# Another order for the change of rounds and the end of a seven-product down projection

## The chip, the cores and the metric

The kernel runs on one core of one Trainium2 chip. The metric is device microseconds (us) of one execution of the program. Five engines work side by side, each in the order of its own queue: TensorE (PE in the profile, with its weight loads as PEld), VectorE (DVE), ScalarE (ACT), GpSimd (POOL) and SyncE (SP), which here issues most DMAs. TensorE writes to PSUM, which has eight banks of 512 fp32 values per partition. The other tiles lie in SBUF.

## The reference

A decoder block on 512 tokens with D = 1024 in fp32: an input projection, sliding-window attention beside a gated linear recurrence, their merge and `w_out`, and then the part that this change touches:

```
h = h + merged @ w_out
u = rmsnorm(h, norm_ffn_g)
z = silu(u @ w_ffn_gate) * (u @ w_ffn_up)        # 512 x 2816
h = h + z @ w_ffn_down                           # 2816 x 1024
return rmsnorm(h, norm_final_g)
```

## The kernel before

**Precision.** Every fp32 product is made of three fast matmuls: each operand is cut into a high half (rounded, made by a copy) and a low half (the remainder, made by a subtraction), and high x high, high x low and low x high are added up in PSUM. For weights the high half `wh` is a copy on ACT (L112) and the low half `wl` a subtraction on DVE (L116).

**Weights.** The class `Weights` brings all weights in as *units* of 1 MB (raw tiles of 128 x 2048, two buffers, loads issued by SP) and cuts each unit into two *slices* (granules in the code) of 128 x 1024, whose halves have three buffers. `get` hands out the next slice and sees that the splits of the next two (`AHEAD`) have been written down before. A split also writes down the load of the next unit. Before a down-projection slice is split, `sums` (L124) adds weight rows on DVE where the method below needs it; in the second round only rows with an even number need it, the first slice of each unit.

**The order on the engines.** The program is written down in one order, and a planner with a cost model of its own decides in which order each engine's queue gets its instructions, by what it believes to be ready when. `tc.issue_after(x)` makes the instructions that stand in its block follow x in the queue of x's engine.

**The FFN.** The rows of h are in `hn` (four token tiles t of 128 rows). For each of the two column halves c of `w_out`, DVE adds the product to hn (L842), PE transposes sixteen 128 x 128 blocks (L845) into PSUM banks `px`, and ACT and DVE write the high and low halves `u2h` (L850) and `u2l` (L851) for k = 4c to 4c + 3. The row factors of the norm are not multiplied in; `row_scale` spreads them with one matmul (L885) into a tile `R`, which is multiplied in later. A projection `fproject` is 24 matmuls (three for each k of 8) from one slice. The hidden width is handled in eleven pairs p = 0..10: `gate(p)` does two projections, `up_(p)` two more and multiplies (`place`, L925), and then builds sums and differences of the parts of z ("forms").

**Seven products.** The down projection treats z and the weights as 2 x 2 blocks (token halves by neighbouring hidden blocks; neighbouring hidden blocks by column halves), and computes the four output blocks from seven block products instead of eight. Each product of a pair p is six matmuls: two token tiles by three. In *round 1*, `round1(p)` accumulates three of them (s3y3, a22y4, s2y2, two banks each) between the projections, over all p. *Round 2* then accumulates the other four (a11b11, n1y1, a12b21, n4b22, two banks each) over p = 0..7, and the loop `tail` does the last three p product by product, so that the output tiles are done one after another. The z forms of round 2, `zh` and `zl`, are kept in SBUF; the forms of round 1 are `f1h`, `f1l`.

**The change of rounds** (L961 to L992). The pool of the projections is given back (L961), a new one is laid over it, two tiles `evs` in it take a copy of s3y3 (ACT), DVE adds a22y4 and s2y2 to hn and to evs, evs is added to hn (four additions, L985 to L987), and then all eight banks are laid out anew for round 2.

**The end.** After each last product, DVE adds it to hn (`onto`, L973; `add_side`, L1035, in pieces of 256 columns), ACT squares the pieces and sums them up. `finish_row(t, late)` multiplies by the gains on POOL (L1044: 512 columns and then 256), reduces on DVE (L1046), takes the power -1/2 on POOL (L1048) and scales by the row's factor: 512 columns on ACT, 256 on DVE (L1050), the last 256 on DVE with the gains (L1051). Then two DMAs write the row tile, one from ACT's queue and one from SP's. Row tiles 2 and 3 are finished first, then 0, then 1.

Of the kernel before, what the change touches and what calls it, by code (L numbers as in the profile page):

```python
# [15 lines left out]
F32 = mybir.dt.float32  # L16
# [6 lines left out]
P = 128  # L23
# [18 lines left out]
class Weights:  # L42


    def __init__(self, nc, pool, units):
        self.nc, self.pool = nc, pool
        self.units = units
        self.raw = {}
        self.grans = []
        for u, (kind, *_rest) in enumerate(units):  # L50
            self.grans += [(u, kind, 0), (u, kind, 1)]
        self.ready = {}
        self.done = 0
        self.pos = 0

    def load(self, u):
# [3 lines left out]
        t = self.pool.tile([P, 2048], F32, tag="raw", bufs=2, name=f"raw{u}")  # L60
# [27 lines left out]
    def split(self, i, pool=None, bufs=3, high=None, low=None, low_after=None):  # L88
        u, kind, half = self.grans[i]
        self.load(u)  # L90
        if u:
            self.load(u + 1)
# [8 lines left out]
        size = 1024  # L101
        if kind in ("r1", "r2"):
# [3 lines left out]
        pool = pool or self.pool  # L106
# [37 lines left out]
def block_kernel(ctx: ExitStack, tc: tile.TileContext, x, norm_mix_g, w_in, b_in,  # L144
# [65 lines left out]
    W = Weights(nc, wpool, units)  # L210
# [176 lines left out]

    def mm3(ps, wh, wl, ah, al):

        for k in range(KD):  # L390
            pe.matmul(ps, wh[:, k, :], ah[:, k, :], start=k == 0, stop=False)  # L391
            pe.matmul(ps, wh[:, k, :], al[:, k, :], start=False, stop=False)  # L392
            pe.matmul(ps, wl[:, k, :], ah[:, k, :], start=False, stop=k == KD - 1)  # L393
# [428 lines left out]
    for c in range(2):  # L822
# [18 lines left out]
        for t in range(NT):  # L841
            tt(hn[:, t, cs], pss[t], hn[:, t, cs], ALU.add)  # L842
            for jj in range(4):
                j = 4 * c + jj
                pe.transpose(px[jj][:, t * P:(t + 1) * P], hn[:, t, j * P:(j + 1) * P], ident)  # L845
            jk = rp.tile([P, S], F32, tag="jk", bufs=2, name="jk")
            act(jk, hn[:, t, cs], AF.Square, accum_out=sq2[:, t, c:c + 1])
        for jj in range(4):
            j = 4 * c + jj
            act(u2h[:, j, :], px[jj], AF.Copy, scale=g_ffn[:, j:j + 1])  # L850
            stt(u2l[:, j, :], px[jj], g_ffn[:, j:j + 1], u2h.bitcast(F32)[:, j, :],  # L851
                ALU.mult, ALU.subtract)
# [13 lines left out]
    psum.release()  # L866
    psum = newpool("psf", "left", bass.MemoryType.PSUM)

    def psg(name):
        return psum.tile([P, S], F32, tag="g", bufs=2, name=name)  # L870

# [4 lines left out]
    rounds1 = {n: [psum.tile([P, S], F32, name=f"{n}_{i}") for i in range(2)]  # L876
               for n in ("s3y3", "a22y4", "s2y2")}
    bc = rounds1["s2y2"][1]
    stream_end = len(W.grans) - 1 - 2 * TAIL_P

    def row_scale():
        diag = fp.tile([P, NT, P], F32, tag="zg", bufs=2, name="diag")
        for t in range(NT):
            dve.tensor_scalar(diag[:, t, :], ident, rstd2[:, t:t + 1], None, ALU.mult)
        pe.matmul(bc, ones, diag.rearrange("p t c -> p (t c)"), start=True, stop=True)  # L885
        dve.tensor_copy(R, bc)

    def fproject(then=None):
        wh, wl = W.get(limit=stream_end)
        ps = psg("ps_f")  # L890
        run(mm3(ps, wh, wl, u2h, u2l))
        if then:
            then()
# [4 lines left out]
    def gate(p):  # L898
        gates_of[p] = []
        for a in range(2):  # L900
            zg = fp.tile([P, S], F32, tag="zg", bufs=2, name="zg")
            tt(zg, fproject(row_scale if p == 0 and a == 0 else None), R, ALU.mult)  # L902
# [9 lines left out]
    def up_(p):  # L912
# [6 lines left out]
        def split(h, l, src):  # L919
            act(h, src, AF.Copy)  # L920
            tt(l, src, h.bitcast(F32), ALU.subtract)

# [6 lines left out]
        if p < NP - 1:  # L929
# [3 lines left out]
            split(h1, l1, z8[:, 4:7, :])  # L933
        else:
            split(h1[:, 2], l1[:, 2], s3)
            place(1)
            split(h1[:, 0], l1[:, 0], a22)
# [12 lines left out]
    def round1(p):  # L950
        h, l = forms1.pop(p)
        for names in (("s3y3",), ("a22y4", "s2y2")):
            wh, wl = W.get(limit=stream_end)
            for b, n in enumerate(names):
                f = dict(a22y4=0, s2y2=1, s3y3=2)[n]
                product(rounds1[n], h[:, f], l[:, f], wh[:, b], wl[:, b],
                        p == 0, p == NP - 1)

    for kind, p in ffn:
# [152 lines left out]
```

## Time and profile before

| | us |
|---|---|
| three runs of before | 909.8, 910.02, 913.58 |
| their median | 910.02 |
| the profiled execution's own time | 911.42 |
| its span, from the first to the last instruction | 909.7 |

All durations below come from that one profiled execution; 1.7 us of its own time lie outside the span. In the views, a row of the timeline has the start, the duration, the engine, the line, the operation, the tile written and the tiles read, and in brackets how long the engine had been idle and what ended it. Rows of the windows have the stretch, its length, busy time and number of instructions of PE, PEld, DVE, ACT and POOL, then the granted TensorE clock (1.00 is full), the busy share of the DMA engines and GB/s. Matmuls overlap: a row's duration reaches from its start to its modelled end, while the next one starts earlier. Rows of the waits have the total, the number and the longest.

### The profile page before, as it was taken

What the parts mean: (1) busy time and instruction counts of PE and PEld (TensorE: products, weight loads), DVE (VectorE), ACT (ScalarE), POOL (GpSimd) and SP (SyncE); (2) the same over time, 40 slices, a digit from 0 to 9 for tenths busy, and PEclk for the clock granted to TensorE, in tenths of its full rate; (3) what the DMA queues carried; (4) which work ended last, traced back from release to release, by engine and by line L of the source; (5) the groups of instructions that cost most, each with busy time, mean ns of one, the idle gap of its engine ahead of it and who ended that gap; (6) DMA issues with size and microseconds to landing.
All of it is one profiled execution on the core that took longest, in us unless ns stands there. A gap on an engine that the chain in (4) does not pass through costs nothing.

```text
span 909.7 us, 11255 instructions
## 1 busy us (share of the span) xinstructions
PE 887.8 (98%) x4410; PEld 749.0 (82%) x4410; DVE 556.6 (61%) x843; ACT 396.6 (44%) x646; POOL 153.4 (17%) x150
## 2 busy tenths in 40 slices
PE   8999999999999999999999999999999999997995
PEld 7988889888898988888888878888888888884874
DVE  5677877647484755745335356565655655667567
ACT  6566775645353545215232342333332333332345
POOL 3004534300000000000000002333322223320005
PEclk9999999999999999999999999999999999997998
DMA  7331211232221141222243222344333343343452
GB/s 257 93 93 47 94 47 47 93 93 93 93 84 56 47 139 47 93 93 92 95 163 114 93 93 93 98 134 139 96 136 121 110 139 116 116 138 116 161 210 94
DMA packets 74642, 97.26 MB, mean 107 GB/s; under 512 B 2042, under 2 KB 64604, under 8 KB 74588
## 3 DMA queue, kind: packets, MB, share of 16 engines
q1 hardware_dynamic: 73996, 95.48, 32.3%
q10 hardware_dynamic: 592, 1.05, 0.3%
q8 instruction: 35, 0.57, 0.3%
q14 instruction: 19, 0.16, 0.0%
HBM read 94.43 MB, written 2.10 MB: 106 GB/s over the span
## 4 chain that ended last, share of the span: by engine, by line
PE 87%; DMA 5%; DVE 4%; SPq 1%; issue 1%; ACT 1%; POOL 0%; DVEq 0%; POOLq 0%; ACTq 0%
PE ps_big L391 13%; PE ps_big L392 13%; PE ps_big L393 13%; PE ps_f L391 8%; PE ps_f L392 8%; PE ps_f L393 8%; DMA raw<-in_w_ffn_down_dram 4%; DVE wl L116 2%; PE ps_v L402 2%; PE ps_v L403 2%; PE ps_v L401 2%; PE ps_o L402 2%; PE ps_o L403 2%; PE ps_o L401 2%; PE pv L527 1%; PE s2y L948 1%
## 5 line engine op out<-in xcount | busy, mean ns | idle before, releaser
L112 ACT ACTIVATE wh<-raw 128x1024 fp32r<-128x1024 f32 (+1 forms) x169 | 173.9, 1032 | 368.2 <-PE ps_f L392 149.1
L116 DVE TENSOR_TENSOR wl<-raw,wh 128x1024 fp32r<-128x1024 f32 (+1 forms) x169 | 211.4, 1252 | 115.7 <-ACT wh L112 115.4
L391 PE MATMUL ps_big<-uh,wh 128*128 128x512 f32 x376 | 148.8, 396 | 0.0
L392 PE MATMUL ps_big<-ul,wh 128*128 128x512 f32 x376 | 147.8, 393 | 0.0
L393 PE MATMUL ps_big<-uh,wl 128*128 128x512 f32 x376 | 147.7, 393 | 0.0
L391 PE MATMUL ps_f<-u2h,wh 128*128 128x512 f32 x352 | 137.4, 390 | 0.0
L393 PE MATMUL ps_f<-u2h,wl 128*128 128x512 f32 x352 | 137.0, 389 | 0.0
L392 PE MATMUL ps_f<-u2l,wh 128*128 128x512 f32 x352 | 136.9, 389 | 0.0
L393 PEld LDWEIGHTS ps_big<-uh,wl 128*128 128x128 f32 x376 | 70.7, 188 | 14.2
L392 PEld LDWEIGHTS ps_big<-ul,wh 128*128 128x128 f32 x376 | 70.8, 188 | 13.6
L391 PEld LDWEIGHTS ps_big<-uh,wh 128*128 128x128 f32 x376 | 70.7, 188 | 13.5
L392 PEld LDWEIGHTS ps_f<-u2l,wh 128*128 128x128 f32 x352 | 66.1, 188 | 13.9 <-issue 0.2
L393 PEld LDWEIGHTS ps_f<-u2h,wl 128*128 128x128 f32 x352 | 66.1, 188 | 13.9
L391 PEld LDWEIGHTS ps_f<-u2h,wh 128*128 128x128 f32 x352 | 66.1, 188 | 13.8 <-issue 0.2
L905 POOL TENSOR_TENSOR zg<-zg,sgf 128x512 f32<-128x512 f32 x22 | 38.9, 1766 | 191.4 <-ACT sgf L162 191.4
L124 DVE TENSOR_TENSOR raw<-raw 128x512 f32<-128x512 f32 x44 | 32.5, 739 | 44.0 <-DMA raw<-in_w_ffn_down_dram 43.6
L285 POOL TENSOR_TENSOR r<-ss,neghalf 128x4 f32<-128x4 f32 x8 | 10.1, 1259 | 232.8 <-DVE ss L284 232.8
L902 DVE TENSOR_TENSOR zg<-ps_f,R 128x512 f32<-128x512 f32 x22 | 15.2, 692 | 37.9 <-PE ps_f L393 37.9
L906 POOL TENSOR_TENSOR zg<-zg,R 128x512 f32<-128x512 f32 x22 | 37.4, 1702 | 1.7
L401 PE MATMUL ps_v<-wh,uh 128*128 128x256 f32 x128 | 36.5, 285 | 0.0
L402 PE MATMUL ps_v<-wl,uh 128*128 128x256 f32 x128 | 36.3, 284 | 0.0
L403 PE MATMUL ps_v<-wh,ul 128*128 128x256 f32 x128 | 36.2, 284 | 0.0
(302 smaller groups left out, 1612.5 us busy)
## 6 DMA issues: line engine op xcount, KB each, us to landing
raw<-in_w_in_dram SPq DMA_DIRECT2D x27, 1024.0 KB, 5.1
raw<-in_w_ffn_gate_dram SPq DMA_DIRECT2D x11, 1024.0 KB, 5.1
raw<-in_w_ffn_up_dram SPq DMA_DIRECT2D x11, 1024.0 KB, 5.2
raw<-in_w_ffn_down_dram SPq DMA_DIRECT2D x11, 1024.0 KB, 4.8
raw<-in_w_ffn_down_dram SPq DMA_DIRECT2D x22, 512.0 KB, 4.2
raw<-in_w_branch_attn_dram SPq DMA_DIRECT2D x4, 1024.0 KB, 5.2
raw<-in_w_branch_hgrn_dram SPq DMA_DIRECT2D x4, 1024.0 KB, 4.7
raw<-in_w_out_dram SPq DMA_DIRECT2D x4, 1024.0 KB, 6.4
```

The source lines that it names most:

```text
L112: nc.scalar.activation(hv, src, AF.Copy)
L116: (low or nc.vector).tensor_tensor(lv, src, hv.bitcast(F32), ALU.subtract)
L124: add = lambda o, i0, i1: self.nc.vector.tensor_tensor(o, i0, i1, ALU.add)
L391: pe.matmul(ps, wh[:, k, :], ah[:, k, :], start=k == 0, stop=False)
L392: pe.matmul(ps, wh[:, k, :], al[:, k, :], start=False, stop=False)
L393: pe.matmul(ps, wl[:, k, :], ah[:, k, :], start=False, stop=k == KD - 1)
L401: pe.matmul(ps, ah[:, k0 + k, ts], wh[:, k, :], start=first and k == 0, stop=False)
L402: pe.matmul(ps, ah[:, k0 + k, ts], wl[:, k, :], start=False, stop=False)
L403: pe.matmul(ps, al[:, k0 + k, ts], wh[:, k, :], start=False, stop=last and k == nk - 1)
L902: tt(zg, fproject(row_scale if p == 0 and a == 0 else None), R, ALU.mult)
L905: pool_e.tensor_tensor(zg, zg, sg, ALU.mult)
L906: pool_e.tensor_tensor(zg, zg, R, ALU.mult)
```

## The change

- **Start of the FFN.** The first two projections get their banks from the old PSUM pool and do k = 0..3 before the last token tile of the second column half is transposed (`turn(NT - 1)`, placed behind the first projection's k = 3). Its u2 halves, `row_scale` (in a bank of the tag "s1") and k = 4..7 follow. The pool is changed when the third projection opens its bank (`open_banks`).
- **Round 1's last pair.** a11b11 of p = 0 stands between s3y3 and a22y4, in the two banks of the projections. The other three products of round 2 take over the banks of s3y3, a22y4 and s2y2. The splits of the first two slices of round 2 are held behind the low half of the s2 form on DVE, that of the second one also behind the last copy of s3y3 on ACT, and that of the third slice behind the last addition of s2y2 to evs (`added`).
- **Evictions.** evs lies in the old pool. The four additions of evs to hn move to p = 1. The last pair's round-2 forms (`rest`) move to p = 2, and then the pool is given back and `gfin` is loaded.
- **Raw buffers.** Units 2, 3, 6, 7 and 10 of round 2 use a second pool `wr` of two raw buffers, which lies where u2 was. With it, a split writes down the loads of the next three units. Two of the last six slices use the ordinary three buffers for their halves and four use the pool `wd`, where all six did.
- **The end.** Squares of 512 columns at once, but for the last side of row tile 1. Row tiles 2, 3 and 0 are scaled on ACT alone (two times 512 columns), POOL multiplies all of their columns by the gains, and both DMAs go out from SP's queue; row tile 1 stays as before.

```
@@ Weights
+        self.more, self.more_units = None, ()
+        self.behind = []
     def load(self, u):
+        if u in self.more_units and self.more is None:
+            return
+        pool = self.more if u in self.more_units else self.pool
+        t = pool.tile([P, 2048], F32, tag="raw", bufs=2, name=f"raw{u}")
     def split(self, i, ...):
-        if u:
-            self.load(u + 1)
+        for v in range(u + 1, u + (4 if self.more else 2 if u else 1)):
+            self.load(v)
...
+        with ExitStack() as order:
+            for ins in self.behind:
+                order.enter_context(self.tc.issue_after(ins))
+            self.cut(i, kind, u, half, raw, src, shape, pool or self.pool, bufs, high, low,
+                     low_after)
@@ start of the FFN
         for t in range(NT):
             tt(hn[:, t, cs], pss[t], hn[:, t, cs], ALU.add)
+            if c == 0 or t < NT - 1:
+                turn(t)
...
+    first = []
+    for a in range(2):
+        wh, wl = W.get()
+        first.append((psb([P, S], "ps_f"), wh, wl))
+        for k in range(4):
+            last_ins = mm3k(*first[a], u2h, u2l, k)
+        if a == 0:
+            with tc.issue_after(last_ins):
+                turn(NT - 1)
+            split_u2()
...
+    row_scale()
+    for ps, wh, wl in first:
+        for k in range(4, KD):
+            mm3k(ps, wh, wl, u2h, u2l, k)
@@ up_(p), last pair
-            split(h1[:, 1], l1[:, 1], s2)
-        tt(n4, a12, s2, ALU.subtract)
-        split(zh[:, p], zl[:, p], z8[:, 0:4, :])
+            W.behind = [split_form(h1[:, 1], l1[:, 1], s2)]
+
+        def rest():
+            tt(n4, a12, s2, ALU.subtract)
+            split_form(zh[:, p], zl[:, p], z8[:, 0:4, :])
+
+        if p < NP - 1:
+            rest()
+        return rest
@@ round1(p)
+        ws = [W.get(limit=first_r2 if last else stream_end) for _ in range(2)]
+        one("s3y3", ws[0], 0)
+        if last:
+            acc["a11b11"] = [banks["g"](f"a11b11_{i}") for i in range(2)]
+            acc["w"] = W.get(limit=first_r2)
+            second("a11b11", 0, acc["w"])
+        one("a22y4", ws[1], 0)
+        one("s2y2", ws[1], 1)
@@ change of rounds
     for i in range(2):
-        ev = dp.tile([P, S], F32, tag="ev", bufs=2, name="ev")
-        act(ev, rounds1["s3y3"][i], AF.Copy)
+        ev = fp.tile([P, S], F32, tag="zg", bufs=2, name="ev")
+        last_copy = raw_ins(act(ev, banks["s3y3"][i], AF.Copy))
         evs.append(ev)
+    W.behind.append(last_copy)
...
+        added = raw_ins(tt(evs[i], banks["s2y2"][i], evs[i], ALU.add))
+    acc.update(n1y1=banks["s3y3"], a12b21=banks["a22y4"], n4b22=banks["s2y2"])
+    wr = newpool("wr", "left")
+    W.more = wr
     for p in range(NP - TAIL_P):
+        w = W.get(limit=stream_end) if p else acc["w"]
+        if p:
+            second("a11b11", p, w)
+        else:
+            W.split(W.done)
+            W.behind = [added]
+            W.split(W.done)
+            W.behind = []
+        second("n1y1", p, w)
+        w = W.get(limit=stream_end)
+        second("a12b21", p, w)
+        second("n4b22", p, w)
+        if p == 1:
+            for i in range(2):
+                onto(2 + i, 1, evs[i])
+                onto(2 + i, 0, evs[i], ALU.subtract)
+        if p == 2:
+            rest()
+            fp.release()
...
     for g in range(2 * TAIL_P):
-        W.split(stream_end + 1 + g, wd, 2 * TAIL_P)
+        if g < 2:
+            W.split(stream_end + 1 + g)
+        else:
+            W.split(stream_end + 1 + g, wd, 4)
@@ finish_row(t, late)
-        for hs in (early, ls):
+        last = t == 1
+        for hs in (early, ls if last else sides[late]):
             pool_e.tensor_tensor(y[:, hs], y[:, hs], gfin[:, hs], ALU.mult)
...
         act(y[:, early], y[:, early], AF.Copy, scale=r1)
-        dve.tensor_scalar(y[:, ls], y[:, ls], r1, None, ALU.mult)
-        stt(y[:, rest], y[:, rest], r1, gfin[:, rest], ALU.mult, ALU.mult)
-        for q, hs in ((nc.scalar, early), (nc.sync, sides[late])):
+        if last:
+            dve.tensor_scalar(y[:, ls], y[:, ls], r1, None, ALU.mult)
+            stt(y[:, rest], y[:, rest], r1, gfin[:, rest], ALU.mult, ALU.mult)
+        else:
+            act(y[:, sides[late]], y[:, sides[late]], AF.Copy, scale=r1)
+        for q, hs in ((nc.scalar if last else nc.sync, early), (nc.sync, sides[late])):
             q.dma_start(out2[t * P:(t + 1) * P, hs], y[:, hs])
```

More of the change, by code (lines that the diff above doesn't have):

```diff
@@ L101, in split, with cut @@
         size = 1024
+        with ExitStack() as order:
[3 more added lines that the diff above has]
+                     low_after)
+    def cut(self, i, kind, u, half, raw, src, shape, pool, bufs, high, low, low_after):
+        nc, size = self.nc, 1024
         if kind in ("r1", "r2"):
@@ L840, in block_kernel, with turn @@
             px = [psb([P, S], "px") for _ in range(3)] + [ps1([P, S], "px")]
[L841 to L842 removed]
+        def turn(t):
             for jj in range(4):
@@ L982, in block_kernel @@
     for i in range(2):
[L983 to L999 removed]
+        onto(i, 1, banks["s2y2"][i])
```

150 lines of the change are left out of this document (76 added, 74 removed).

## Prediction

> **What bounds it now.** I read the page first, then the busy time by windows, the waits of PE, and the timeline at each place where PE stood still.
>
> ```profile
> span 909.7 us, 11255 instructions
> ...
> PE 887.8 (98%) x4410; PEld 749.0 (82%) x4410; DVE 556.6 (61%) x843; ACT 396.6 (44%) x646; POOL 153.4 (17%) x150
> ...
> PEclk9999999999999999999999999999999999997998
> ...
> PE 87%; DMA 5%; DVE 4%; SPq 1%; issue 1%; ACT 1%; POOL 0%; DVEq 0%; POOLq 0%; ACTq 0%
> ```
>
> TensorE is the bound: 98% busy, 87% of the chain. No matmul is removed, so only idle PE time and slow PE clock can be won. The clock row shows one dip, in slices 37 and 38 of 40; the windows and PE's waits say where.
>
> ```profile
> 842.00:882.00 40.00, 40.00 (x178) 33.12 (x177) 22.50 (x22) 15.89 (x15) 0.00 (x0) 1.00 0.53 179
> ...
> 824.14:841.78 17.64, 10.96 (x26) 7.13 (x25) 14.23 (x26) 4.99 (x7) 0.00 (x0) 0.61 0.32 113
> ...
> 826.63:828.03 1.40, 1.24 (x5) 0.71 (x5) 1.40 (x4) 0.90 (x1) 0.00 (x0) 1.00 0.00 0
> 828.03:829.90 1.87, 1.18 (x2) 0.46 (x2) 1.87 (x3) 0.42 (x1) 0.00 (x0) 0.50 0.00 0
> ...
> PE a11b L948 <- ACT ev L157: 3.7, 1, 3.7
> ...
> PE a22y L948 <- ACT f1h L157: 2.1, 1, 2.1
> ...
> PE px L845 <- DVE hn L842: 0.8, 1, 0.8
> ...
> PE a11b L1014 <- DVE wl L116: 0.8, 1, 0.8
> ```
>
> In a full stretch (first row) 178 matmuls touch 40 us, two of them only its ends: 40/176.6 = 0.2265 us each. Between 824.14 and 841.78, the change of rounds, 25 matmuls start (one s3y3, six each of a22y4, s2y2, a11b11, n1y1; 26 touch it). At full pace they need 25 x 0.2265 = 5.7 us of the 17.64: **12.0 us lost**, by idle time and by a granted clock of 0.50 from 828.03 on. The other two waits are the boundary to the FFN (px) and the last products (L1014); behind PE's last matmul comes the end of the kernel.
>
> **The change, part by part.** *A, start of the FFN.*
>
> ```profile
> 539.02 1.03 PE L845 MATMUL px<-ident,hn 128*128 128x128 f32 x8
> ...
> 540.09 1.28 DVE L842 TENSOR_TENSOR hn<-ps_o,hn 128x512 f32<-128x512 f32 x2
> ...
> 540.83 1.25 PE L845 MATMUL px<-ident,hn 128*128 128x128 f32 x8 [0.78 <-DVE hn L842]
> ...
> 541.84 0.47 PE L391 MATMUL ps_f<-u2h,wh 128*128 128x512 f32 x1
> ...
> 542.11 2.40 ACT L157 ACTIVATE u2h<-px,prm 128x512 fp32r<-128x512 f32 x4
> ...
> 542.82 1.41 DVE L851 SCALAR_TENSOR_TENSOR u2l<-px,prm,u2h 128x512 fp32r<-128x512 f32 x2
> ```
>
> The sixteen transposes take 541.84 - 539.02 = 2.82 us, against 2 x 1.03 for two groups like the first: 0.8 us is waiting for hn, and some 0.3 more restarting behind it. After the change 24 matmuls on k = 0..3 (two projections, 5.4 us) need only what the first column half left, so PE has work. The last token tile's transposes move behind twelve of them, to about 543.6; its u2h then takes 2.4 us on ACT and its u2l 4 x 0.71 us on DVE, plus the diagonal that DVE already writes there, ending near 548.3. PE asks for k = 4 at about 547.2 and for k = 7 two microseconds later, so each is there in time. The row-scale matmul is the same, in a freed "s1" bank. If that cover failed, late u2l would cost what is won. Gain 0 to 1.1; I take **1.0**.
>
> *B, the change of rounds.*
>
> ```profile
> 822.78 0.39 PE L393 MATMUL ps_f<-u2h,wl 128*128 128x512 f32 x1
> ...
> 824.84 0.69 DVE L124 TENSOR_TENSOR raw<-raw 128x512 f32<-128x512 f32 x1 [3.53 <-DMA raw<-in_w_ffn_down_dram]
> ...
> 825.45 0.68 DVE L925 TENSOR_TENSOR z<-ps_f,zg 128x512 f32<-128x512 f32 x1
> ...
> 826.05 1.22 DVE L116 TENSOR_TENSOR wl<-raw,wh 128x1024 fp32r<-128x1024 f32 x1
> ...
> 826.17 0.42 ACT L157 ACTIVATE f1h<-z 128x256 fp32r<-128x256 f32 x1 [2.08 <-DVE z L925]
> ...
> 826.49 1.04 ACT L112 ACTIVATE wh<-raw 128x1024 fp32r<-128x1024 f32 x1
> ...
> 826.64 0.50 PE L948 MATMUL a22y<-wh,f1h 128*128 128x512 f32 x1 [2.11 <-ACT f1h L157]
> ...
> 834.66 1.22 DVE L921 TENSOR_TENSOR zl<-z,zh 128x1024 fp32r<-128x1024 f32 x1
> ...
> 835.91 1.09 ACT L157 ACTIVATE ev<-s3y 128x512 f32<-128x512 f32 x2 [1.93 <-DVE zl L921]
> ...
> 836.56 0.80 PE L948 MATMUL a11b<-wh,zh 128*128 128x512 f32 x1 [3.72 <-ACT ev L157]
> ```
>
> The last up projection ends at 822.78 + 0.39 = 823.2, yet the product that reads it (L925) starts at 825.45: DVE's queue is headed by a weight sum (L124) that waits for a DMA. That is PE's first gap, 2.27 us from 824.37 to 826.64. The second is the bank: a11b11 waits for ev, and ev, in a pool laid over the old one, for zl.
>
> After the change DVE has no weight work of round 2 in front of the forms. L925 starts at 823.2, f1h 0.72 later (825.45 to 826.17) at 823.9, a22y4 another 0.47 later at 824.4, just as s3y3 ends (824.14 + 0.23). The s2 form needs two subtractions, a copy and a low half, about 0.45 each: done near 825.7. PE does a22y4 and s2y2 to 824.4 + 12 x 0.2265 = 827.1.
>
> The added wait: behind the s2 form's low half, DVE now holds the first round-2 slice's sum (0.69) and low half (1.22); ACT's high half (1.04) needs the sum; a11b11 and n1y1 on PE need all three. Sum to 826.4, high to 827.5 (828.15 if ACT takes the odd row's slice first), low 1.2 later. PE idles 0.4 to 1.0 us, with up to 0.35 more for the low half. Next, the first slice of unit 1 is held behind `added`, behind six evictions of 0.64 (1.28 for two hn additions in A's rows; 3.8 us) and two low halves (2.4 us): from 826.4 that is 832.6, up to 833.1 with the waits between them; then sum and high, 834.3 to 835.0. PE's 24 matmuls from 827.5 end near 833.4. So p = 1 starts at 834.3 to 835.0 instead of 841.78 + 12 x 0.2265 = 844.5. With no idle time it would be 832.5. Of the 12.0 us some 1.8 to 2.5 stay: gain **9.9**, between 9.5 and 12.0.
>
> What moves: four additions of evs to p = 1 (4 x 0.64 = 2.6 us of DVE) and the last z forms to p = 2 (a 256-wide subtraction of about 0.42 and a low half of 1.22 on DVE, a high half of about 1.04 on ACT). In the full stretch above DVE is busy 22.5 of 40 us, ACT 15.9, so about 7 us of DVE are free in the 16 us that take these 4.2; cost nothing, and up to 2 us if they push a low half out of its turn. On SP, the loads of units 2 and 3 go out once u2h is free (823.2) instead of waiting for a split; gfin stands behind them until the old pool is free, with four raw buffers (4 x 24 x 0.2265 = 21.7 us of PE work) as cover.
>
> *C, last products.*
>
> ```profile
> 883.73 0.39 PE L1014 MATMUL a11b<-wh,zl 128*128 128x512 f32 x1
> ...
> 885.77 0.40 PE L1014 MATMUL a11b<-wh,zl 128*128 128x512 f32 x1
> ...
> 881.64 5.14 DMA raw<-in_w_ffn_down_dram
> ...
> 886.81 1.07 ACT wh L112
> ```
>
> From 883.73 to 885.77 three matmuls start in 2.04 us that need 0.68: **1.4** lost to late splits, behind loads that wait for two raw buffers (the chain shows one from 881.64). With four, unit 10's load can go when unit 6 is split, some 6 us ahead of need. Gain 0 to 1.4; I take 1.4.
>
> *D, the end.*
>
> ```profile
> 900.07 0.39 PE L1014 MATMUL n4b<-wh,zl 128*128 128x512 f32 x1
> ...
> 899.69 0.75 POOL L1044 TENSOR_TENSOR hn<-hn,gfin 128x256 f32<-128x256 f32 x1 [1.50 <-ACT jkd L157]
> ...
> 900.90 1.27 POOL L1044 TENSOR_TENSOR hn<-hn,gfin 128x512 f32<-128x512 f32 x1
> ...
> 900.97 0.72 ACT L157 ACTIVATE hn<-hn,r1d 128x512 f32<-128x512 f32 x1 [0.16 <-POOL r1d L1048]
> ...
> 900.97 1.35 DVE L1050 TENSOR_SCALAR hn<-hn,r1d 128x256 f32<-128x256 f32 x1 [0.77 <-POOL r1d L1048]
> ...
> 902.64 0.74 DVE L1035 TENSOR_TENSOR hn<-n4b,hn 128x256 f32<-128x256 f32 x2
> ...
> 904.93 0.35 DVE L1050 TENSOR_SCALAR hn<-hn,r1d 128x256 f32<-128x256 f32 x1 [0.75 <-POOL r1d L1048]
> ```
>
> PE's last result is there at 900.46, but DVE adds it at 902.64: it first scales row 0, where one L1050 takes 1.35 us beside a POOL multiplication that ends at 902.17, against 0.35 without one (904.93). Row 0 goes to ACT, so the add can start 2.1 us earlier. What is late next: POOL multiplies 512 columns where it did 256 for three rows (1.27 - 0.75 = 0.5 each), and row 0's two ACT scalings (1.44) stand before the last squares. From that add to row 1's scaling are 904.93 - 902.64 = 2.29 us of squares, reduction and power; from 900.5 on they end at 902.8 if nothing stands between them, and at 903.2 to 903.9 if row 0's scalings hold the squares back by one (0.72, in part) or both. So 1.0 to 1.7 us; I take **1.2**, bounds 2.1 gained and 0.6 lost (POOL's 1.5 added in full on top of 0.9 kept).
>
> Sum: 1.0 + 9.9 + 1.4 + 1.2 = **13.5 us**. The profiled execution took 911.42 (span 909.7 and 1.7 around it), 1.4 above the median of 910.02; so 897.9 in its terms, **896.5** as a median.
>
> **Rivals.** *One half-clock stretch remains.* A mean clock of 0.61 over the 17.64 us, with 3.89 at 1.00, leaves 0.50 for all the rest: 13.75 us. If B's remaining idle time trips it again in dense work, 13.75/2 = 6.9 us go: 903.4. Against: gaps of 1.0 us (540) and 1.4 us in two parts (884) left the clock alone, and I expect 1.0 at a time; it took a 2.27 us gap here. The Trainium skill, "TensorE: Matmul & The Clock Gate", Part 1, has the clock halve only after an idle window of about 3.4 us. By that rule this rival falls away and its chance goes to the forecast; the trace disagrees, since 2.27 us was enough, and the trace decides.
>
> *ScalarE and POOL become the end.* Row 0's scaling delays the last squares and POOL's added 3 x 0.5 us shows: D costs 0.6 instead of gaining 1.2, 898.3. The Trainium skill, "ScalarE: Activation LUTs", Rules for kernel authors, is on this side: it gives multiplications to VectorE, not ScalarE. The rows are against it where POOL runs: 1.35 for 256 columns on DVE, 0.72 for 512 on ACT.
>
> *It doesn't do what it says*: PE's order keeps a11b11 before a22y4. PE then waits from 824.37 to 827.5, over the 2.27 that tripped the clock, and B gains nothing: only A, C and D count, 906.4.
>
> *Slower*: the clock keeps closing. Round 2 is dense, so each stretch costs 6.9 us; two eat all 13.5 (910.3), a third gives 896.5 + 20.7 = 917.2. It decides from three stretches on. For it: two idle spots 6 us apart; against: the one stretch before was not followed by another.
>
> **How the numbers follow.** Forecast 0.68, one stretch 0.13, end bound 0.08, no effect at B 0.07, slower 0.04. A measurement of this kernel tells about 0.5%, 4.6 us, from no change. Faster 0.68 + 0.13 + 0.08 = 0.89, same 0.07, slower 0.04. Low end: B whole, A 1.1, D 2.1, so 1.1 + 12.0 + 1.4 + 2.1 = 16.6 gained, 893.4; high end the one-stretch rival, 903.4; outside it stay 0.11.
>
> **What would show it.** Right: PE clock 1.00 through the change of rounds, no PE gap over 1.1 us there, p = 1 ten microseconds earlier, L925 within 0.5 us of the last up-projection matmul, no L1014 wait, L1050 only once and at 0.35. Wrong: a clock of 0.50 near 828; DVE's queue headed by a weight sum waiting for a DMA (units 2 and 3 are not held back by order); PE waiting for `wh` over 2 us; POOL without idle time after 895.

## The result and the profile after

| | before | after |
|---|---|---|
| median of four runs | 909.91 us | 903.85 us |
| lowest to highest | 909.77 to 913.58 | 903.16 to 904.19 |
| ratio, 95% interval | | 0.9923, 0.9897 to 0.9948 |
| the profiled execution's span | 909.7 us | 902.1 us |

By the medians the change makes the kernel faster by 6.1 us, 0.7%. The ratio in the table, 0.8% (0.5 to 1.0%), is that of the means, in which before's run of 913.58 counts. The forecast was 896.5 within 893.4 to 903.4: the sign held, the size was less than half, and the time lies 0.45 us above the range.

From the page of the changed kernel, to be read against the page of before:

```profile
span 902.1 us, 11238 instructions
...
PE 886.8 (98%) x4410; PEld 747.6 (83%) x4410; DVE 550.6 (61%) x836; ACT 396.9 (44%) x635; POOL 154.1 (17%) x150
...
PEclk9999999999999999999999999999999999999999
...
PE 91%; DMA 3%; DVE 3%; SPq 1%; issue 1%; ACT 0%; POOL 0%; POOLq 0%; DVEq 0%; ACTq 0%
```

The dip of the clock in slices 37 and 38 is gone from the page, and PE's share of the chain has grown from 87 to 91%. A slice is 22.6 us long, so the clock row can't show a short stretch. The windows of the changed kernel can; the last column but two is the granted clock:

```profile
823.25:836.51 13.26, 9.50 (x30) 6.21 (x29) 13.05 (x22) 5.69 (x8) 0.00 (x0) 0.87 0.49 175
...
826.09:829.50 3.41, 2.23 (x9) 1.08 (x7) 3.41 (x6) 1.96 (x2) 0.00 (x0) 1.00 0.89 344
829.50:832.92 3.42, 0.99 (x2) 0.37 (x2) 3.42 (x5) 0.86 (x1) 0.00 (x0) 1.00 0.02 8
832.92:836.33 3.41, 3.25 (x8) 2.61 (x9) 3.41 (x6) 0.19 (x1) 0.00 (x0) 0.50 0.13 29
...
868.00:880.00 12.00, 11.38 (x46) 8.05 (x46) 9.99 (x9) 7.47 (x8) 0.00 (x0) 1.00 0.26 88
```

In the first row 29 matmuls start (30 touch it). They need 29 x 0.2265 = 6.6 us and take 13.26: **6.7 us are still lost** at the change of rounds, where 12.0 were lost before. From 829.50 to 832.92 PE starts two matmuls, and the 3.41 us behind that run at a clock of 0.50. In the last row 46 matmuls touch the twelve microseconds that hold 54 at full pace (the last row of *turned_tail_free* below): 54 - 46 = 8 matmuls, or 1.8 us, are lost among the last products, where 1.4 were.

What PE waited for from 815 us on, first; then VectorE's and PE's rows of the timeline at the change of rounds:

```profile
PE s2y L1002 <- DVE ev L1054: 2.0, 2, 1.3
PE a11b L1002 <- DVE wl L129: 1.5, 2, 1.2
PE a11b L1002 <- ACT wh L125: 0.5, 1, 0.5
...
```

```profile
822.38 0.69 DVE L969 TENSOR_TENSOR z<-ps_f,zg 128x512 f32<-128x512 f32 x1 [2.82 <-PE ps_f L405]
...
824.36 0.42 DVE L987 TENSOR_TENSOR z<-z 128x256 f32<-128x256 f32 x1
824.93 0.43 DVE L996 TENSOR_TENSOR f1l<-z,f1h 128x256 fp32r<-128x256 f32 x1 [0.15 <-ACT f1h L170]
825.27 0.68 DVE L137 TENSOR_TENSOR raw<-raw 128x512 f32<-128x512 f32 x1
825.88 0.68 DVE L1042 TENSOR_TENSOR hn<-hn,a22y 128x512 f32<-128x512 f32 x1
826.47 0.68 DVE L137 TENSOR_TENSOR raw<-raw 128x512 f32<-128x512 f32 x1
827.08 0.68 DVE L1042 TENSOR_TENSOR hn<-hn,a22y 128x512 f32<-128x512 f32 x1
827.67 1.22 DVE L996 TENSOR_TENSOR zl<-z,zh 128x1024 fp32r<-128x1024 f32 x1
828.81 0.68 DVE L1042 TENSOR_TENSOR hn<-hn,s2y 128x512 f32<-128x512 f32 x1
...
830.60 0.68 DVE L1054 TENSOR_TENSOR ev<-s2y,ev 128x512 f32<-128x512 f32 x1
831.20 0.68 DVE L137 TENSOR_TENSOR raw<-raw 128x512 f32<-128x512 f32 x1
831.80 1.22 DVE L129 TENSOR_TENSOR wl<-raw,wh 128x1024 fp32r<-128x1024 f32 x1
```

```profile
821.89 0.39 PE L405 MATMUL ps_f<-u2h,wl 128*128 128x512 f32 x1
...
827.15 0.73 PE L1002 MATMUL a11b<-wh,zh 128*128 128x512 f32 x2 [0.52 <-ACT wh L125]
...
828.19 0.65 PE L1002 MATMUL a22y<-wh,zh 128*128 128x512 f32 x2
830.15 0.50 PE L1002 MATMUL s2y<-wh,zh 128*128 128x512 f32 x1 [1.30 <-DVE ev L1054]
831.34 0.49 PE L1002 MATMUL s2y<-wh,zh 128*128 128x512 f32 x1 [0.70 <-DVE ev L1054]
833.08 0.80 PE L1002 MATMUL a11b<-wl,zh 128*128 128x512 f32 x1 [1.24 <-DVE wl L129]
```

(In the lines on PE, a11b, s3y, a22y and s2y on zh are a11b11, n1y1, a12b21 and n4b22 of round 2: the banks keep their old names.) VectorE never stops from 824.93 on. It has the forms done early, as forecast, and place(1) (L969) starts as soon as its product is there. But the low half of round 2's first slice (L129) comes at 831.80, behind ten other instructions. Six are the reads of the banks. One is the slice's own sum. The other three were not expected there: the sum of unit 2 (826.47), the low half zl of the last pair (827.67), which the program writes down at p = 2, and the sum of unit 1 (831.20). The planner had pulled them forward. PE has the high-half products of both slices put first, then stands in front of s2y2's banks at 828.7 and 830.4, and in front of the low half at 831.6.

### The profile page after: what moved, and what is told of

It reads as the page before. It is cut to its first block, busy times and chain, and to the rows that moved or that the text cites. A ratio compares the mean times of both kernels' runs of the same rounds, so it can differ in the third digit from the quotient of the medians.

```text
span 902.1 us, 11238 instructions
## 1 busy us (share of the span) xinstructions
PE 886.8 (98%) x4410; PEld 747.6 (83%) x4410; DVE 550.6 (61%) x836; ACT 396.9 (44%) x635; POOL 154.1 (17%) x150
## 4 chain that ended last, share of the span: by engine, by line
PE 91%; DMA 3%; DVE 3%; SPq 1%; issue 1%; ACT 0%; POOL 0%; POOLq 0%; DVEq 0%; ACTq 0%
PE ps_big L405 13%; PE ps_big L403 13%; PE ps_big L404 13%; PE ps_f L404 9%; PE ps_f L405 9%; PE ps_f L403 9%; DMA raw<-in_w_ffn_down_dram 3%; PE ps_v L420 2%; PE ps_v L421 2%; PE ps_v L419 2%; PE ps_o L420 2%; PE ps_o L421 2%; PE ps_o L419 2%; DVE wl L129 2%; PE s2y L1002 2%; PE a22y L1002 2%
## 5 line engine op out<-in xcount | busy, mean ns | idle before, releaser
L129 DVE TENSOR_TENSOR wl<-raw,wh 128x1024 fp32r<-128x1024 f32 (+1 forms) x169 | 209.5, 1245 | 107.2 <-ACT wh L125 106.2
```

What stands on the lines that cost most here:

```text
L129: (low or nc.vector).tensor_tensor(lv, src, hv.bitcast(F32), ALU.subtract)
```

## The experiments

All are edits of the changed kernel, and all compute the whole output. In the count of the whole weight stream, which the expectations use, units 0 to 10 of round 2 are units 74 to 84 and their slices 148 to 169. The ratio is against before, run beside them on the same chip (its medians there are 909.38 to 909.79, beside after 909.91, so a difference to after's median can be off by half a microsecond); "lost" is what PE's steps from one matmul to the next have above 0.2265 us, where that is over 0.08 us, and so a little less than the counts above; "end" is from the start of the last matmul to the end of the span.

| kernel | median us | ratio, 95% interval | lost 820-860 | lost 860-885 | end |
|---|---|---|---|---|---|
| before | 909.91 | | 12.0 | 1.2 | 9.6 |
| after | 903.85 | 0.9923 (0.9897 to 0.9948) | 6.5 | 1.6 | 7.7 |
| rest_late | 899.55 | 0.9894 (0.9878 to 0.9911) | 4.1 | 0.1 | 7.7 |
| sums_late | 901.71 | 0.9916 (0.9901 to 0.9931) | 4.8 | 1.0 | 7.6 |
| evict_late | 900.82 | 0.9906 (0.9892 to 0.9921) | 4.8 | 0.8 | 7.7 |
| splits_free | 898.44 | 0.9881 (0.9866 to 0.9896) | 3.8 | 0.4 | 7.6 |
| sums_in_turn | 903.75 | 0.9937 (0.9923 to 0.9952) | 3.9 | 3.7 | 8.3 |
| all_turned | 898.93 | 0.9882 (0.9868 to 0.9897) | 0.0 | 2.1 | 9.0 |
| turned_tail_free | 895.07 | 0.9839 (0.9823 to 0.9856) | 0.0 | 0.0 | 7.6 |
| turned_scaling_dve | 894.96 | 0.9842 (0.9827 to 0.9857) | 0.0 | 0.0 | 7.5 |
| two_raw | 903.15 | 0.9927 (0.9910 to 0.9943) | 7.3 | 0.8 | 8.4 |
| scaling_on_dve | 903.21 | 0.9930 (0.9915 to 0.9945) | 7.3 | 0.8 | 7.6 |
| small_squares | 903.50 | 0.9933 (0.9918 to 0.9948) | 6.5 | 1.4 | 8.3 |
| old_end | 903.79 | 0.9938 (0.9921 to 0.9954) | 6.7 | 1.1 | 7.7 |

The three losses come from one trace each. How much of that is chance, *scaling_on_dve* shows: VectorE and PE have the same order as in after at the change of rounds, and yet 7.3 us are lost in place of 6.5, because two stretches of 3.41 us at half clock follow in place of one.

The theory to test was that VectorE's order sets the start of round 2, and that whatever stands ahead of the first low half and of the reads of s2y2 is paid in full. The rivals: loads or ScalarE set it; the half clock alone costs.

**rest_late** holds the last pair's remaining forms back:

```
-                onto(2 + i, 0, evs[i], ALU.subtract)
+                held = onto(2 + i, 0, evs[i], ALU.subtract)
...
-            rest()
+            with tc.issue_after(held):
+                rest()
```

> The last pair's n4 and four forms (rest) are held behind the four additions of evs, on VectorE. Theory 1 (VectorE's own order sets the start of round 2: everything that stands ahead of the last two reads of s2y2 and of the first slice's low half is paid in full): zl with 1.15 us a step leaves that place, so the first low half starts at about 830.65 instead of 831.80 and the time falls by 1.1 to 1.2 us to 902.7; if the three gaps of PE also become short enough that no half clock follows, by another 1.6 us (eight products at 0.426 instead of 0.2265 us) to 901.1. Rival 2 (the loads or ScalarE's high halves set the start): no change, 903.9. Rival 3 (only the half clock costs, the gaps are hidden): no change or 902.3.

4.3 us less, more than any theory had. By the traces the change of rounds gave 2.4 of it, close to the 2.8 of the case without a half clock, which is indeed gone. The other 1.5 came from the last products, where nothing had been expected; *sums_in_turn* is about them.

**sums_late** holds the splits of units 75 to 77 behind the first low half:

```
+            low148 = W.low_ins
             W.split(W.done)
-            W.behind = [added]
+            W.behind = [added, low148]
             W.split(W.done)
-            W.behind = []
...
         if p == 1:
+            W.behind = []
```

(`low_ins` is the instruction of the last low half written down.)

> The splits of units 75, 76 and 77 (sum, high and low half) are held behind the low half of the first slice as well as behind the last read of s2y2. Theory 1: the sums of units 76 and 75 (0.60 us a step each) leave the place ahead of the first low half, which starts at about 830.6 instead of 831.8; 1.2 us less, 902.65, or 901.05 without the half clock; the three sums then stand ahead of the second slice's low half, which starts at 833.5 as before. Rival 2 (loads or ScalarE): no change, 903.9. A third outcome is that the third slice's high half, now behind sum 75 at about 832.4, comes too late and gives 0.5 us of it back.

2.1 us less, again without a half clock, between the two values given.

**evict_late** puts the first low half ahead of the reads of s2y2:

```
+    with tc.issue_after(W.low_ins):
         for i in range(2):
             onto(i, 1, banks["s2y2"][i])
             added = raw_ins(tt(evs[i], banks["s2y2"][i], evs[i], ALU.add))
```

> The four instructions that read s2y2 are held behind the low half of the first slice; the sum of unit 76 and the rest of the last pair still stand ahead of it. PE's order changes with it: the eight low products of the first slice come ahead of the two high ones into s2y2's banks. Theory 1: low half from 828.8 instead of 831.8, the eight products from 830.0; the banks of s2y2 free at 831.2 and 832.4; the third slice's high half, behind the sum of unit 75, at about 834: gaps of 0.7, 1.3, 0.4 and 1.4 us in place of 0.7, 1.5, 1.0 and 1.5 with a half clock of 1.6: about 2.4 us less, 901.4 (or 903.1 if a half clock stays). Rival 2 (the banks of s2y2 set the start, since round 2 needs them): these come 1.15 us later, so 1 us slower, 904.9.

3.0 us less, though s2y2's banks come free later: the banks are not the bound by themselves, their place in VectorE's queue is. All three edits take only a different piece out of the same queue, and each gains. The rival that loads or ScalarE alone set the start falls.

**splits_free** undoes one part of the change, the holds of round 2's first splits behind the s2 form, the copies of s3y3 and the reads of s2y2:

```
-            W.behind = [split_form(h1[:, 1], l1[:, 1], s2)]
+            split_form(h1[:, 1], l1[:, 1], s2)
...
-    W.behind.append(last_copy)
...
-            W.behind = [added]
```

> Undoes one part of the change: nothing holds the weight splits behind the forms, the copies or the reads of the banks. VectorE then cuts the first slice between place(1) and the form a22, the second between a22 and s2, and PE has all twelve products of the first slice of round 2 ahead of a22y4. Theory 1 in its wide form (PE idles because the first slice is cut too late; it has nothing else to do while VectorE makes the forms and reads the banks): 2 to 4 us less, about 901. The change's own reason (splits ahead of the forms make the forms late): the forms come 1.2 us later each, place(1) behind the sum of unit 75 that lands at about 823.5 another 1 us: 1 to 3 us more, about 906.

5.4 us less. The part that was to make the start of round 2 early cost that much: with the first slice cut early, PE has its twelve products to do while VectorE makes the forms. What still stands in the way shows in VectorE's timeline of this run:

```profile
823.90 0.69 DVE L137 TENSOR_TENSOR raw<-raw 128x512 f32<-128x512 f32 x1 [3.66 <-DMA raw<-in_w_ffn_down_dram]
824.51 0.68 DVE L969 TENSOR_TENSOR z<-ps_f,zg 128x512 f32<-128x512 f32 x1
825.11 1.21 DVE L129 TENSOR_TENSOR wl<-raw,wh 128x1024 fp32r<-128x1024 f32 x1
```

The sum of unit 1 waits 3.66 us for its load ahead of place(1), the very head-of-queue wait that the prediction read in before. PE waits 1.7 us for it.

**sums_in_turn** holds each sum of round 2 behind the low half that stands before it in the program:

```
-            self.sums(u, half, raw)
+            with self.tc.issue_after(self.low_ins) if kind == "r2" else nullcontext():
+                self.sums(u, half, raw)
```

> One edge more than after: the sum of a unit of the down projection's second round stands on VectorE behind the low half of the slice before it, so in the order of the text, all the way to the end; the holds behind the forms stay. Theory for the last products (VectorE waits at a sum written two units ahead for a load that only starts when its own next low half frees the raw buffer, 12.9 us in six waits from 838 to 867, one trip a unit of 5.6 us against 5.44 us of PE, so it never gains a lead): the load of the last unit goes out several us before 868.76 and PE's excess steps from 871 to 879 (1.65 us) fall to 0.3 or less. At the change of rounds the sums of units 76 and 75 leave the place ahead of the first low half, as in sums_late: 2.2 to 3 us less. Sum: 899.5, range 898.5 to 901. Rival (the raw and slice buffers alone limit the lead): the excess at the end stays at 1.2 us or more, 901.

No change in sum, where 899.5 was expected, for two reasons of opposite sign. For the line of the sums from 836 to 870 us, the idle time of VectorE in front of it by what ended it, in after and in rest_late:

```profile
its engine sat idle before it (us, times) until:
  DMA raw<-in_w_ffn_down_dram: 12.9, 6
```

```profile
its engine sat idle before it (us, times) until:
  DMA raw<-in_w_ffn_down_dram: 8.7, 5
```

In after the planner has put each sum ahead of the second low half of a unit three before it, and that low half frees the raw buffer for a load that a later sum waits for. So VectorE goes round once a load and gains no lead on PE. In *sums_in_turn* the view has no such idle time at all, and the last unit's load goes out at 862.37 in place of 868.76.

The change of rounds gained 2.6 us. But the edge went too far: the sums of the last units now stood behind slices that wait for a buffer, PE waited for slice 166 twice, and a half clock followed:

```profile
874.18:877.60 3.42, 1.85 (x8) 0.98 (x7) 2.30 (x3) 2.99 (x4) 0.00 (x0) 1.00 0.00 0
877.60:881.01 3.41, 3.41 (x10) 2.63 (x9) 3.41 (x3) 1.39 (x2) 1.27 (x1) 0.50 0.00 0
```

So the expected gain at the end was taken back by a new wait, the miss of this run.

**all_turned** joins the edits of *splits_free*, *rest_late* and *sums_in_turn*.

> The three causes taken away together: no splits held behind the forms (as in splits_free), the last pair's rest behind the four additions of evs (as in rest_late), each sum of the second round behind the low half before it (as in sums_in_turn). VectorE then goes place(1), n1, low half of slice 0, form a22, s2, low half of slice 1, sum 75, form s2, the reads of the banks with the third low half among them. Theory 1: the stall of 1.87 us that the sum of unit 75 made ahead of place(1) in splits_free goes, PE idles at most 1 us between 822 and 845 and under 0.4 us from 868 to 880: 896.5, range 895.7 to 897.7. Rival (the gains overlap, since all of them only use the same idle time of PE): 898, no better than splits_free with 898.44.

The time is the rival's, 898.9, but not for the rival's reason. At the change of rounds everything came true, and the loss is the one of *sums_in_turn* among the last products. **turned_tail_free** takes that away:

```
-        self.low_ins = getattr(ins, "ins", ins)
+        if i < len(self.grans) - 8:
+            self.low_ins = getattr(ins, "ins", ins)
```

> all_turned with one difference: from the last three units on (81 to 83) the sums stand behind the low half of slice 161, not each behind the slice before it, so that the splits of units 83 and 84 need not wait for the last slice of unit 82. all_turned lost 0.98 and 1.03 us at two products of the tail while PE waited for slice 166, and VectorE came to the first result 3 us late because it still cut slices 166 to 169 until 876.5. Theory: those two steps go (2.0 us), VectorE is through with its splits by about 870, and the stretch from the last matmul to the end returns from 8.6 to 7.3 us as in rest_late: 898.93 less 2.0 less 1.0 to 1.3 gives 895.7, range 895.0 to 897.0. Rival (GpSimd and ScalarE hold the end, whatever PE does): 1 us less or nothing, 898 to 899.

895.07, at the lower edge of what was expected. The same two windows of *all_turned* and of *turned_tail_free*:

```profile
822.00:845.00 23.00, 23.00 (x103) 19.07 (x102) 21.39 (x37) 11.72 (x14) 0.00 (x0) 1.00 0.74 267
868.00:880.00 12.00, 10.43 (x45) 8.11 (x44) 9.93 (x11) 7.35 (x11) 4.61 (x3) 1.00 0.00 0
```

```profile
822.00:845.00 23.00, 23.00 (x103) 19.04 (x102) 21.38 (x37) 10.94 (x13) 0.00 (x0) 1.00 0.77 276
868.00:880.00 12.00, 12.00 (x54) 9.94 (x54) 9.14 (x14) 4.64 (x10) 5.81 (x5) 1.00 0.00 0
```

PE is busy without a break through the change of rounds in both, 103 matmuls in 23 us, and in the second also among the last products. This version is 8.8 us faster than the changed kernel by the medians; against its own runs of before the ratio is 0.9839.

**two_raw** goes back to two raw buffers:

```
-    W.more_units = [len(units) - NP + q for q in range(NP) if q % 4 > 1]
...
-    wr = newpool("wr", "left")
-    W.more = wr
```

> Undoes one part of the change: two raw buffers in place of four. The load of unit 76 then waits for the second low half of unit 74 (833.5 to 834.7), lands at about 839 and its high half is there at 841, with PE busy on units 74 and 75 until about 842.5; after that two units a cycle of load (4.5), sum (0.6), high half (1.0) and two low halves (2.3), 8.4 us against 10.9 us of PE. Theory: the extra buffers bring nothing in the middle, and VectorE's waits at the sums, not their number, make the lead: 903.9 to 904.5. Rival (the change's reason: the buffers give the lead): the loss from 868 to 880 grows from 1.65 us by 1 us or more, 905 or more.

No difference that can be told; the loss from 868 to 880 did not grow. Its trace is of its slowest run (905.18; the others took 902.58 to 903.22). In after the buffers bring no time that can be told, though the last unit's load goes out 25.6 us ahead of the last matmul there and 15.9 us ahead of it in *two_raw*. Whether they matter once VectorE does not wait at its sums (*turned_tail_free*) was not tried.

**scaling_on_dve**, **small_squares** and **old_end** undo the end of the change:

```
-        last = t == 1
+        last = True
```

```
-    def square(t, c, n=2):
+    def square(t, c, n=1):
-    def add_side(t, side, src, n=2):
+    def add_side(t, side, src, n=1):
...
-        square(2 + i, 0)
+        for c in range(2):
+            square(2 + i, c)
```

> Undoes one part of the end of the change: all four rows scale their last half as the second row does (256 columns on VectorE, 256 with gfin in one VectorE operation, the first half's store on ScalarE's queue), as before the change. Prediction's step D (row scaling on VectorE meets GpSimd's work and takes 1.35 us instead of 0.35 us): from the last matmul to the end 8.3 to 8.9 us instead of 7.75, so 904.4 to 905.0. Rival (only the last row counts, and that is scaled on VectorE in both): no change, 903.9.

> Undoes one part of the end on the changed kernel: the additions into the rows and their squares in pieces of 256 columns again (two of 0.33 us a step in place of one of 0.6 on VectorE, two of 0.6 with their read of the accumulator in place of one of 0.8 on ScalarE). Theory: with the scaling acquitted by scaling_on_dve, the gain of 1.9 us from the last matmul to the end lies here, since VectorE and ScalarE came so late in before that its last add stood 2.1 us behind the last product: 904.5 to 905.8. Rival (the gain lies neither here nor in the scaling, but in what is ready earlier because the splits and loads end earlier): within 0.4 us of 903.85.

> Undoes both parts of the end on the changed kernel at once: scaling of all rows as before the change (as in scaling_on_dve) and additions and squares in pieces of 256 columns (as in small_squares). Each alone cost nothing. Theory (either one is enough to keep the last row's additions out of the way of a 1.35 us scaling beside GpSimd): with neither, the last addition stands about 2 us behind the last product again, as in before, where 0.4 to 0.8 us were seen in after and in the two runs, and the time is 904.9 to 905.8. Rival (the 1.9 us at the end came from neither, but from splits and loads that ended earlier or from chance in the order): 903.2 to 904.2.

None of the three costs anything that the time tells, and *old_end* has both edits. (*small_squares* has an end of 8.3 us in its one trace, 0.6 more than after; its median does not show it.) The timeline of *old_end* at the last addition:

```profile
892.81 0.35 DVE L1138 TENSOR_SCALAR hn<-hn,r1d 128x256 f32<-128x256 f32 x1 [0.39 <-POOL r1d L1135]
...
893.08 0.48 DVE L1139 SCALAR_TENSOR_TENSOR hn<-hn,r1d,gfin 128x256 f32<-128x256 f32 x1
...
893.31 1.38 POOL L1131 TENSOR_TENSOR hn<-hn,gfin 128x512 f32<-128x512 f32 x1 [0.54 <-ACT jkd L170]
...
893.70 0.76 DVE L1121 TENSOR_TENSOR hn<-s2y,hn 128x256 f32<-128x256 f32 x2
```

VectorE scales row 0 here too, but in 0.35 us: it starts half a microsecond before GpSimd's multiplication and is over when that begins. **turned_scaling_dve** asks the same of the fast version:

> turned_tail_free with the scaling of all rows as before the change (256 columns each by VectorE, which spares GpSimd 0.6 us and ScalarE 0.7 us a row on three rows). Theory: in scaling_on_dve this cost nothing on a PE that idles; with PE's idle time gone GpSimd and ScalarE have less slack, so it is equal or up to 0.7 us faster than turned_tail_free: 895.0 to 895.7. Rival (the 1.35 us scaling beside GpSimd that made the last add of before late comes back once the results follow each other without idle time): 1 to 2 us slower, 896.7 to 897.7.

894.96 against 895.07: equal, here too.

## Why the prediction was right and wrong

**A, the start of the FFN: mis-sized, 0.3 of 1.0 us.** The last up projection's last matmul starts at 821.89 in after and at 822.78 in before, 0.9 us earlier. But 0.55 of that is there already at the last matmul of `w_out`, ahead of the change; in the thirteen traces of the changed kernel and its edits that one starts anywhere from 537.75 to 539.22. From it to the last up projection's last matmul are 283.99 us in before and 283.65 in after (283.64 to 283.68 in all thirteen): 0.34 us gained. PE's rows in before, then in after:

```profile
538.79 0.39 PE L403 MATMUL ps_o<-wh,ml 128*128 128x512 f32 x1
```

```profile
538.24 0.39 PE L421 MATMUL ps_o<-wh,ml 128*128 128x512 f32 x1
...
544.59 1.04 PE L863 MATMUL px<-ident,hn 128*128 128x128 f32 x8
545.38 0.48 PE L405 MATMUL ps_f<-u2h,wl 128*128 128x512 f32 x1
546.07 0.73 PE L403 MATMUL ps_f<-u2h,wh 128*128 128x512 f32 x2 [0.21 <-ACT u2h L170]
```

The step that failed is "The last token tile's transposes move behind twelve of them, to about 543.6", and with it "so each is there in time". The transposes of two token tiles (x8) went behind 23 matmuls, to 544.59. The wait for hn is gone, but PE now comes too early to the new u2 halves: its two steps from 545.38 on take 0.69 and 0.34 us in place of 0.23. A was not undone by itself.

**B, the change of rounds: the mechanism right, the remainder mis-sized.** The prediction left 1.8 to 2.5 of 12.0 us and took 9.9 as the gain; 6.7 stayed and 5.3 were gained. Its first half held: place(1) at once, a22y4 right behind s3y3, PE idle 0.4 to 1.0 us ahead of a11b11 (0.68 as a step). The steps that failed are two. *"low 1.2 later"* and *"up to 0.35 more for the low half"* set the first low half directly behind its high half, at 827.5 to 828.2; it came at 831.80. And *"cost nothing, and up to 2 us if they push a low half out of its turn"* priced the moved forms by VectorE's mean free time over 16 us, at p = 2, where they are written down; the planner issued them ahead of the reads and the low half that PE was waiting for. *rest_late* shows that this one piece cost 4.3 us in the end, 2.4 of them here. That sums of later units could head VectorE's queue the prediction had named ("units 2 and 3 are not held back by order"), without a price. It also took PE's products slice by slice; in after all high halves stand first, so that PE was out of work sooner.

That the holds behind the forms were worth having was taken from the change, not from the profile. *splits_free* shows that undoing them gains 5.4 us. By the rows of before, the forms were PE's wait there because a sum that waited for a load stood ahead of them, not because of the splits that are cut from loads already there.

**The rival of one half-clock stretch (903.4) came true in kind, not in price.** One stretch remained, and the time is near its number. But it lasted 3.41 us and cost some 1.6 us, 0.2 a step; the price of 6.9 was from four such stretches in a row in before. That it was one and not two is chance, by *scaling_on_dve*. The rest of the shortfall is idle time.

**C, the last products: wrong.** Of 1.4 us nothing was gained; 1.8 are lost. "unit 10's load can go when unit 6 is split, some 6 us ahead of need" took the number of buffers for what limits the lead. The load did go earlier, 25.6 us ahead of the last matmul in place of 18.8. But PE starved from 871.7 on for low halves that VectorE made late (867.51 to 872.22), behind a sum that had waited 2.28 us for its own load. *two_raw* shows that the number is indifferent, *rest_late*, *sums_in_turn* and *turned_tail_free* that the order decides.

**D, the end: the size nearly right, the cause wrong.** 9.6 us became 7.7, 1.9 by unrounded times, where 1.2 was taken. Three pieces make it up. The last addition starts 2.57 us behind the start of the last matmul in before and 0.43 in after, the 2.1 us of the prediction. From it to row 1's scaling on VectorE 2.3 us became 2.9, because ScalarE's scalings of row 0 hold the last squares back, as it had feared. From there to the end 4.8 became 4.4, which it had not counted.

But it was not the scaling's place that brought the addition forward: with the scaling moved back to VectorE, and with all of the end undone, it starts at 0.43 as well, and the ends are 7.6 and 7.7. Moving the scaling loses 0.5 us ahead of row 1's scaling and gains 0.4 behind it (2.4 and 4.8 in *scaling_on_dve*), so undoing it costs nothing. What differs from before in all these runs is how early VectorE is through with its splits; its rows in before, then in after:

```profile
887.90 1.23 DVE L116 TENSOR_TENSOR wl<-raw,wh 128x1024 fp32r<-128x1024 f32 x1 [0.26 <-ACT wh L112]
889.04 1.28 DVE L973 TENSOR_TENSOR hn<-hn,a11b 128x512 f32<-128x512 f32 x2
```

```profile
875.48 3.49 DVE L129 TENSOR_TENSOR wl<-raw,wh 128x1024 fp32r<-128x1024 f32 x3
881.12 1.28 DVE L1042 TENSOR_TENSOR hn<-hn,a11b 128x512 f32<-128x512 f32 x2 [2.15 <-ACT v L170]
```

The last split ends 10.9 us ahead of the last matmul (900.07) in before and 15.4 us ahead of it (894.35) in after. In before VectorE reaches the first result only when its splits are done, and GpSimd's multiplications, which follow from there, come beside the scaling of row 0. That this is the cause is argued and not shown, since no run has the old end with late splits. The nearest pair agrees in the number alone: in *all_turned* the splits end 10.2 us ahead and the end is 9.0; in *turned_tail_free* 15.5 us ahead and 7.6. But in *all_turned* the last addition starts at 0.43 too, and it is the last squares that wait for ScalarE's scalings; and *small_squares* has 15.4 us and an end of 8.3. What made the splits end early is, by its one trace, the four raw buffers: in *two_raw*, without them, they end 8.8 us ahead, and the end is 8.4, though the median does not show it.

In sum, by the traces: 0.3 + 5.3 - 0.4 + 1.9 = 7.1 us, and with the 0.55 us ahead of the change the 909.7 - 902.1 = 7.6 us between the spans. The medians are only 6.1 us apart, because the traced run of before (911.42) is 1.5 us above its median; where in before those 1.5 us lie no trace shows.

## What to carry to other kernels

Where a planner orders the queues, an instruction's place in the program is no place in time: what is moved "to later" may be issued first, so price it at the worst moment at which its inputs are ready, or tie it down with an edge, and read the queue of the engine that PE waits for, not its mean load. A wait for a load that stands in an in-order queue ahead of the instruction that frees the next load's buffer turns buffers into nothing; look for it before adding more. And when a wait at a boundary has two parties, give PE the work that needs neither before hurrying one of them.

## What the runs showed of the hardware

The half clock follows a rule sharper than the idle gap that the prediction argued with. In all fourteen traces the granted clock changes only on a grid of 3.413 us that is fixed within an execution and starts at another phase in each. Taking 0.2265 us for every 512-column matmul and less in proportion for narrower ones, every full-clock window from 30 us on (the start, with matmuls of other forms, is left out) in which PE's matmuls fill 0.38 or less (21 of them, the idle ones at the very end among them) is followed by a window at 0.50, and every one with 0.41 or more (3,514 of them) by one at full clock:

| kernel | window from | share of matmuls | clock of the next |
|---|---|---|---|
| after | 829.50 | 0.13 | 0.50 |
| before | 824.61 | 0.28 | 0.50 |
| scaling_on_dve | 827.76 | 0.34 | 0.50 |
| sums_in_turn | 874.18 | 0.38 | 0.50 |
| turned_scaling_dve | 884.33 | 0.41 | 1.00 (PE was done) |
| all_turned | 871.15 | 0.43 | 1.00 |
| evict_late | 832.26 | 0.43 | 1.00 |
| rest_late | 827.13 | 0.47 | 1.00 |

*all_turned* and *sums_in_turn* have the same two waits of 1.0 us there, and only the second lost its clock: the phase of the grid put them at 0.43 and 0.38. In the windows of before, the stretch goes on while work at half pace fills little of a window, and ends behind the one that is full:

```profile
824.61:828.03 3.42, 1.24 (x5) 0.71 (x5) 3.19 (x6) 1.37 (x2) 0.00 (x0) 1.00 0.15 59
828.03:831.44 3.41, 2.71 (x6) 1.71 (x7) 3.24 (x6) 0.89 (x2) 0.00 (x0) 0.50 0.40 106
...
838.27:841.68 3.41, 3.41 (x9) 2.64 (x9) 2.38 (x4) 0.00 (x0) 0.00 (x0) 0.50 0.06 24
841.68:845.09 3.41, 3.41 (x16) 2.81 (x16) 1.23 (x1) 1.44 (x2) 0.00 (x0) 1.00 0.00 0
```

The Trainium skill, "TensorE: Matmul & The Clock Gate", Part 1, gives a free-running window of 3413 ns; the grid agrees. It closes the clock after an idle window; here windows with up to 0.38 of work closed it too.
